# Stepping the start addresses of the activation buffers in a two-layer decoder trunk

## The chip, the cores and the metric

The kernel runs on one NeuronCore of a Trainium2 chip. Its five engines are TensorE (PE in the profile, with its weight loads shown apart as PEld), VectorE (DVE), ScalarE (ACT), GpSimd (POOL) and SyncE (SP). The metric is the device time of one execution in microseconds (us), given as the median over several runs.

## What is computed

The reference is a trunk of two decoder layers over 256 tokens of width 2048. Layer 0 mixes tokens by retention (8 heads), layer 1 by sliding-window attention (32 query heads, 4 key heads). A gated convolutional feed-forward block follows each:

```python
def reference(x, ...):
    h = x
    for i in range(DEPTH):
        hn = rmsnorm(h, norm_mix_g[i])
        h = h + (retention(...) if i % 2 == 0 else sliding_window_attention(...))
        hn = rmsnorm(h, norm_ffn_g[i])
        h = h + conv_ffn(hn, ffn_w_up[i], ffn_conv_w[i], ffn_conv_b[i], ffn_w_down[i])
    return rmsnorm(h, final_norm_g)
```

All of it is float32. Nearly all the arithmetic is in the products of 256 tokens with weight matrices: 2048 x 12288 and 4096 x 2048 for retention, 2048 x 2560 and 2048 x 2048 for attention, and 2048 x 11008 and 5504 x 2048 in each feed-forward block.

## The kernel before

Each float32 operand of a large product is split into a high part and a remainder, so that a product becomes three matmuls in TensorE's fast float32 type: high by high, high by remainder, remainder by high.

**Weights.** A unit of weights is 1 MB (128 partitions x 2048 floats, a few chunks of 128 rows side by side). A DMA from SyncE brings it into one of three `raw` buffers. ScalarE copies it to `hi` (line 156) and VectorE writes the remainder to `lo` (line 157), four buffers of each, in pieces of 1024 columns. `run_main` walks through the units in one fixed order, loads five units ahead and splits about three ahead.

**Activations.** They are held transposed, a chunk of 128 features by 256 tokens at a time, high part and remainder side by side: 512 floats, 2048 bytes in each partition. The norm's chunks are the 16 buffers `xT`, made in `halves` (lines 306 and 310). The gated chunks of the feed-forward blocks are 18 buffers `zT`, made at the end of `ffn_tile` (lines 596 to 600). The mixers' output chunks are `yT`.

**Two forms of the product.** `products` (lines 243 to 245) has the activation as stationary operand: a weight load reads 128 of its columns, 512 bytes of each partition, and the matmul then streams 512 columns of `hi` or `lo`. It serves the down-projections, the output projections and the retention's values and gates. `products_tr` (lines 254 and 256) has it the other way round: 128 columns of `hi` or `lo` are loaded as stationary operand, and the activation streams past. For each chunk of activations this is a block of four matmuls: two of 512 columns (line 254) and two of 256 (line 256). It serves queries, keys and the up-projections. In attention, line 380 loads 64 columns of the values `vs` as stationary operand (`vc` picks them: the first of two heads at a multiple of 512 bytes, the second 256 bytes past one) and streams 256 or 128 columns of `pT`.

**Where buffers lie.** The pools are laid out one above the other in each partition: constants, `acts` (the `xT` buffers), `wp` (`raw`, `hi`, `lo`), `st` (small tiles), and a pool per phase (`zT`, `yT`, `u`, `cv`, the heads' tiles). A tile `free` of 40 floats, which nothing uses, stands at the end of the constants. In the program as built, every buffer of `xT`, `zT`, `yT`, `raw`, `hi` and `lo` starts at a multiple of 512 bytes, and so do the slices that weight loads and matmuls of the two product forms read.

Of the kernel before, what the change touches and what calls it, by code (L numbers as in the profile page):

```python
# [9 lines left out]
F32 = mybir.dt.float32  # L10
F32R = mybir.dt.float32r
# [5 lines left out]
P = 128  # L17
D = 2048
S = 256
NT = S // P  # L20
NC = D // P
# [86 lines left out]
class Kernel:  # L108
# [178 lines left out]
    def squares(self, p):  # L287
# [8 lines left out]
                nc.gpsimd.tensor_tensor(out=self.acc, in0=self.acc, in1=sq[:, i], op=ALU.add)  # L296
        yield 0

    def halves(self, norm, at):

        nc = self.nc
        made = []
        for c, src in at:
            g = self.gT[:, norm * NC + c : norm * NC + c + 1]
            x = self.acts.tile([P, 2, S], F32R, tag="xT", name="xT", bufs=NC)
            nc.scalar.activation(out=x[:, 0], in_=src, func=AF.Copy, scale=g)
            made.append((src, g, x))
            self.xT[c] = x
        for src, g, x in made:
            nc.vector.scalar_tensor_tensor(  # L310
                out=x[:, 1], in0=src, scalar=g, in1=x[:, 0].bitcast(F32),
                op0=ALU.mult, op1=ALU.subtract,
            )
# [261 lines left out]
    def ffn_tile(self, zT, layer, f, u):  # L575
        nc = self.nc
        c = self.ph.tile([P, 2, S], F32, tag="cv", name="cv", bufs=2)
        for half in range(2):
            w = self.cw[:, layer, f + half * NF]
            nc.scalar.activation(  # L580
                out=c[:, half], in_=u[:, half], func=AF.Identity, scale=w[:, 2:3], bias=w[:, 3:4]
            )
        yield 1
        for half in range(2):
            w = self.cw[:, layer, f + half * NF]
            for d in (1, 2):
                nc.vector.scalar_tensor_tensor(  # L587
                    out=c[:, half, d:], in0=u[:, half, : S - d], scalar=w[:, 2 - d : 3 - d],
                    in1=c[:, half, d:], op0=ALU.mult, op1=ALU.add,
                )  # L590
        yield 1
        nc.scalar.activation(out=c[:, 0], in_=c[:, 0], func=AF.Silu)
        yield 1
        s = c[:, 0]
        nc.vector.tensor_tensor(out=s, in0=s, in1=c[:, 1], op=ALU.mult)
        z = self.ph.tile([P, 2, S], F32R, tag="zT", name="zT", bufs=18)
        nc.scalar.copy(out=z[:, 0], in_=s)
        if f + 1 not in F_CUTS:
            yield 1
        nc.vector.tensor_tensor(out=z[:, 1], in0=s, in1=z[:, 0].bitcast(F32), op=ALU.subtract)  # L600
        zT[f] = z
# [190 lines left out]
    def run(self):  # L792
        nc, a, const = self.nc, self.a, self.const
        self.ph_ctx = None
        self.ident = const.tile([P, P], F32, name="ident")
        make_identity(nc, self.ident)
        self.ones = const.tile([P, P], F32, name="ones")
        nc.gpsimd.memset(self.ones, 1.0)
        self.mhalf = const.tile([P, NT], F32, name="mhalf")
        nc.gpsimd.memset(self.mhalf, -0.5)  # L800
        nc.scalar.copy(out=self.mhalf, in_=self.mhalf)
        self.h = const.tile([P, NC, S], F32, name="h")
        self.htok = self.h.rearrange("p c (t d) -> p t c d", t=NT)
        self.gT = const.tile([P, 4 * NC], F32, name="gT")
        nc.sync.dma_start(out=self.gT, in_=a["gT"])
        self.cw = const.tile([P, 2, 2 * NF, 4], F32, name="cw")
        self.bT = const.tile([P, 18], F32, name="bT")
        self.bv = const.tile([P, 256], F32, name="bv")
        self.sinks = const.tile([P, KV * GRP], F32, name="sinks")

        const.tile([P, 40], F32, name="free")

        self.plan_retention()
        self.plan_ffn(0)
        self.plan_attention()
        self.plan_ffn(1)

        self.open_phase("ret")
        self.units[0].groups[0].begin = None
        for c0, c1, n in ((0, 2, 1), (2, 4, 3), (4, 8, 4), (8, 12, 6), (12, 16, 7)):  # L820
            nc.sync.dma_start(out=self.h[:, c0:c1], in_=a["xT"][:, c0:c1])
            self.load_to(n)
        for p, n in ((0, 1), (1, 3), (2, 4), (3, 4)):
            self.norm_halves(0, p)
            self.split_to(n)
        for p, at in enumerate(NORM_AT, 4):
            self.add(self.norm_pair(0, p), at)
        for p in range(NC // 2):
            self.add(self.squares(p), SQUARES[0] + p * SQUARES[1])
        self.add(self.norm_scale(2), SCALE_AT)  # L830
        self.add(self.constants(), 2)
        self.add(self.tokens(), TOKENS_AT)
        self.run_main()
        self.ph_ctx.close()
# [107 lines left out]
```

## Time and profile before

| | |
|---|---|
| median of 3 runs | 2447.19 us (2446.1 to 2448.56) |
| the profiled execution | 2445.04 us, span 2442.9 us |
| granted TensorE clock, mean | 0.998 |
| PE busy | 2425.2 us, 99% of the span |
| DVE, ACT, POOL busy | 64%, 50%, 1% |
| DMA engines busy, by slice of the span | 4 to 7 tenths, 188 GB/s |

The span goes from the first instruction to the last. A matmul's recorded duration is longer than its share of the engine's time, since matmuls overlap; what a matmul costs is read from the distance between the starts of two that follow each other. PEld rows are weight loads, which run beside the matmul before them.

### The profile page before, as it was taken

To read this page: it belongs to the slowest core of one execution; us is meant where nothing else is said; L and a number is where in the kernel's file an instruction comes from. 1 tells how busy PE (TensorE), PEld (TensorE's weight loads), DVE (VectorE), ACT (ScalarE), POOL (GpSimd) and SP (SyncE) were. 2 spreads that over 40 slices of the span, in tenths; PEclk is the share of its full clock that TensorE was granted. 3 is DMA by queue.
4 is the path that set the end of the run, shared out by engine and by line. 5 is a ranking of instruction groups with operands and counts; after the bars stand their busy time and mean duration, and the time that the engine had idled before them with its cause. 6 is when DMAs were issued, how large, how long until landed. Compare 5 with 4: busy or idle time off the path is not lost.

```text
span 2442.9 us, 31366 instructions
## 1 busy us (share of the span) xinstructions
PE 2425.2 (99%) x12676; PEld 2063.1 (84%) x12676; DVE 1554.8 (64%) x2104; ACT 1225.2 (50%) x1782; POOL 28.9 (1%) x37
## 2 busy tenths in 40 slices
PE   8999999999999999999999999999999999999998
PEld 6888888888888888888888888888888888888887
DVE  6555555554556775677577756876777477657774
ACT  5444344344445553555455545765555355535553
POOL 3000000000000000000000000000000000000000
PEclk9999999999999999999999999999999999999999
DMA  7655555555554555555555555445555555554553
GB/s 270 218 185 185 184 189 180 187 187 182 181 194 168 196 183 193 193 191 180 199 191 192 191 184 193 182 155 194 174 190 174 206 190 190 190 206 174 192 199 127
DMA packets 68977, 460.27 MB, mean 188 GB/s; under 512 B 8032, under 2 KB 9184, under 8 KB 16736
## 3 DMA queue, kind: packets, MB, share of 16 engines
q1 hardware_dynamic: 68544, 457.23, 52.6%
q8 instruction: 99, 1.62, 0.3%
q10 hardware_dynamic: 288, 1.05, 0.1%
q14 instruction: 46, 0.38, 0.0%
HBM read 456.15 MB, written 2.10 MB: 188 GB/s over the span
## 4 chain that ended last, share of the span: by engine, by line
PE 97%; DMA 1%; POOL 1%; issue 1%; ACT 0%; DVE 0%; POOLq 0%; SPq 0%; ACTq 0%
PE mm L254 33%; PE mm L256 17%; PE mm L243 15%; PE mm L245 15%; PE mm L244 15%; PE po L380 1%; PE ms L263 1%; DMA raw<-in_ret_in 1%; PE ms L665 1%; POOL acc L296 1%; PE ms L489 0%; DMA h<-in_xT 0%; DVE lo L157 0%; PE ms L354 0%; ACT hi L156 0%
## 5 line engine op out<-in xcount | busy, mean ns | idle before, releaser
L157 DVE TENSOR_TENSOR lo<-raw,hi 128x1024 fp32r<-128x1024 f32 (+1 forms) x849 | 1017.2, 1217 | 601.2 <-ACT hi L156 600.8
L254 PE MATMUL mm<-xT,hi 128*128 128x512 f32 x3552 | 1120.5, 397 | 6.2 <-DVE xT L310 6.2
L156 ACT CAST hi<-raw 128x1024 fp32r<-128x1024 f32 (+1 forms) x849 | 858.0, 1042 | 514.3 <-PE mm L245 290.8
L256 PEld LDWEIGHTS mm<-xT,lo 128*128 128x128 f32 x3552 | 667.7, 188 | 159.5 <-DVE lo L157 2.2
L256 PE MATMUL mm<-xT,lo 128*128 128x256 f32 x3552 | 699.3, 278 | 0.6 <-DVE lo L157 0.6
L254 PEld LDWEIGHTS mm<-xT,hi 128*128 128x128 f32 x3552 | 543.7, 189 | 11.6 <-ACT hi L156 6.2
L243 PE MATMUL mm<-hi,zT 128*128 128x512 f32 x688 | 268.3, 390 | 0.0
L245 PE MATMUL mm<-hi,zT 128*128 128x512 f32 x688 | 267.7, 389 | 0.0
L244 PE MATMUL mm<-lo,zT 128*128 128x512 f32 x688 | 267.7, 389 | 0.0
L243 PE MATMUL mm<-hi,xT 128*128 128x512 f32 (+1 forms) x544 | 212.0, 390 | 2.1 <-DVE q L366 2.1
L245 PE MATMUL mm<-hi,xT 128*128 128x512 f32 (+1 forms) x544 | 209.1, 384 | 0.0
L244 PE MATMUL mm<-lo,xT 128*128 128x512 f32 (+1 forms) x544 | 209.1, 384 | 0.0
L587 DVE SCALAR_TENSOR_TENSOR cv<-u,cw,cv 128x255 f32<-128x255 f32 x344 | 158.3, 481 | 6.1
L243 PE MATMUL mm<-hi,yT 128*128 128x512 f32 x384 | 153.2, 399 | 0.0
L245 PEld LDWEIGHTS mm<-hi,zT 128*128 128x128 f32 x688 | 129.1, 188 | 26.9
L243 PEld LDWEIGHTS mm<-hi,zT 128*128 128x128 f32 x688 | 129.1, 188 | 26.5
L244 PEld LDWEIGHTS mm<-lo,zT 128*128 128x128 f32 x688 | 129.2, 188 | 26.4
L245 PE MATMUL mm<-hi,yT 128*128 128x512 f32 x384 | 149.8, 390 | 0.0
L244 PE MATMUL mm<-lo,yT 128*128 128x512 f32 x384 | 149.7, 390 | 0.0
L365 ACT COPY u<-mm 128x512 f32<-128x512 f32 x86 | 50.4, 586 | 192.9 <-PE mm L256 192.9
L366 DVE TENSOR_TENSOR u<-mm,u 128x512 f32<-128x512 f32 x86 | 59.5, 692 | 101.8 <-ACT u L365 101.8
L243 PEld LDWEIGHTS mm<-hi,xT 128*128 128x128 f32 x544 | 102.7, 189 | 21.9 <-DVE q L366 2.3
(112 smaller groups left out, 1402.5 us busy)
## 6 DMA issues: line engine op xcount, KB each, us to landing
raw<-in_up SPq DMA_DIRECT2D x172, 1024.0 KB, 4.7
raw<-in_ret_in SPq DMA_DIRECT2D x94, 1024.0 KB, 4.7
raw<-in_dn SPq DMA_DIRECT2D x72, 1024.0 KB, 4.8
raw<-in_ret_out SPq DMA_DIRECT2D x32, 1024.0 KB, 4.7
raw<-in_qkv SPq DMA_DIRECT2D x20, 1024.0 KB, 4.7
raw<-in_att_out SPq DMA_DIRECT2D x14, 1024.0 KB, 4.8
raw<-in_dn SPq DMA_DIRECT2D x16, 512.0 KB, 3.3
raw<-in_dn SPq DMA_DIRECT2D x8, 768.0 KB, 4.3
```

The source lines that it names most:

```text
L156: nc.scalar.copy(out=hi, in_=raw)
L157: nc.vector.tensor_tensor(out=lo, in0=raw, in1=hi.bitcast(F32), op=ALU.subtract)
L243: nc.tensor.matmul(out, lhsT=ah, rhs=hi, start=first, stop=False)
L244: nc.tensor.matmul(out, lhsT=ah, rhs=lo, start=False, stop=False)
L245: nc.tensor.matmul(out, lhsT=al, rhs=hi, start=False, stop=last)
L254: nc.tensor.matmul(out, lhsT=hi[:, sl], rhs=both, start=first, stop=False)
L256: nc.tensor.matmul(out[:, :S], lhsT=lo[:, sl], rhs=act[:, 0], start=False, stop=last)
L263: self.nc.tensor.transpose(out=ps[:, j * P : (j + 1) * P], in_=x, identity=self.ident)
L296: nc.gpsimd.tensor_tensor(out=self.acc, in0=self.acc, in1=sq[:, i], op=ALU.add)
L365: nc.scalar.copy(out=x, in_=g.ps[:, :, S:])
L366: nc.vector.tensor_tensor(out=x, in0=g.ps[:, :, :S], in1=x, op=ALU.add)
L587: nc.vector.scalar_tensor_tensor(out=c[:, half, d:], in0=u[:, half, : S - d], scalar=w[:, 2 - d : 3 - d], in1=c[:, half, d:], op0=ALU.mult ...
```

## The change

Each `xT` and each `zT` buffer is made 4 floats (16 bytes) longer than its 512 floats, and the kernel uses the first 512 of them. A tile `gap` of 64 floats (256 bytes) is set ahead of the `xT` buffers. The scratch memory for software-generated DMA descriptors is cut from 16,384 to 1,024 bytes a partition, which frees the room.

```diff
+    def stepped(self, pool, tag, bufs):
+
+        x = pool.tile([P, 2 * S + 4], F32R, tag=tag, name=tag, bufs=bufs)
+        return x[:, : 2 * S].rearrange("p (x s) -> p x s", x=2)
...
-            x = self.acts.tile([P, 2, S], F32R, tag="xT", name="xT", bufs=NC)
+            x = self.stepped(self.acts, "xT", NC)
...
-        z = self.ph.tile([P, 2, S], F32R, tag="zT", name="zT", bufs=18)
+        z = self.stepped(self.ph, "zT", 18)
...
         const.tile([P, 40], F32, name="free")
+        self.acts.tile([P, 64], F32, name="gap")
...
-    nc = bacc.Bacc("TRN2", target_bir_lowering=False, num_devices=1)
+    nc = bacc.Bacc(
+        "TRN2", target_bir_lowering=False, num_devices=1, dynamic_dma_scratch_size=1024
+    )
```

The instructions of every engine, their order and their waits are the same in both programs. Only addresses differ. In the program as built the pool rounds each buffer up to a multiple of 32 bytes, so that the 2064 bytes take 2080, and neighbours are 32 bytes further past a multiple of 512, not 16. Addresses below are bytes within a partition; the residue is what is left over a multiple of 512:

```
buffers        first address, residue, pitch before    first address, residue, pitch after
xT (16)            41472      0       2048                 26368     256       2080
raw (3)            74240      0       8192                 59648     256       8192
hi (4)             98816      0       8192                 84224     256       8192
lo (4)            131584      0       8192                116992     256       8192
zT (18)           178688      0       2048                164096     256       2080
yT, attention     204288      0       2048                189696     256       2048
```

After the change, then, all buffers of weights start 256 bytes past a multiple of 512, and the k-th `xT` or `zT` buffer starts 32k bytes further round than they do: the first at the same residue as the weights, the next 32 bytes on, and so on round the circle of 512 once in 16 buffers. `yT` keeps the residue of the weights.

## Rows read from the trace of the kernel before

**Rows 1.** The page, part 1: busy time, share and instructions.
```profile
PE 2425.2 (99%) x12676; PEld 2063.1 (84%) x12676; DVE 1554.8 (64%) x2104; ACT 1225.2 (50%) x1782; POOL 28.9 (1%) x37
```

**Rows 2.** The page, part 4: chain that ended last, by engine.
```profile
PE 97%; DMA 1%; POOL 1%; issue 1%; ACT 0%; DVE 0%; POOLq 0%; SPq 0%; ACTq 0%
```

**Rows 3.** The waits of PE: total us, times, longest us.
```profile
PE mm L254 <- DVE xT L310: 6.2, 1, 6.2
PE mm L243 <- DVE q L366: 2.1, 1, 2.1
PE mm L256 <- DVE lo L157: 0.6, 2, 0.4
```

**Rows 4.** The page, part 5, groups: busy us, mean ns, idle us before, releaser.
```profile
L157 DVE TENSOR_TENSOR lo<-raw,hi 128x1024 fp32r<-128x1024 f32 (+1 forms) x849 | 1017.2, 1217 | 601.2 <-ACT hi L156 600.8
L254 PE MATMUL mm<-xT,hi 128*128 128x512 f32 x3552 | 1120.5, 397 | 6.2 <-DVE xT L310 6.2
L256 PE MATMUL mm<-xT,lo 128*128 128x256 f32 x3552 | 699.3, 278 | 0.6 <-DVE lo L157 0.6
...
L243 PE MATMUL mm<-hi,zT 128*128 128x512 f32 x688 | 268.3, 390 | 0.0
...
L243 PE MATMUL mm<-hi,xT 128*128 128x512 f32 (+1 forms) x544 | 212.0, 390 | 2.1 <-DVE q L366 2.1
...
L243 PE MATMUL mm<-hi,yT 128*128 128x512 f32 x384 | 153.2, 399 | 0.0
```

**Rows 5.** Windows: us; PE busy (instructions); granted clock; DMA share; GB/s.
```profile
1000.00:1050.00 50.00, 50.00 (x289) 1.00 0.49 170
1160.00:1190.00 30.00, 30.00 (x134) 1.00 0.54 207
```

**Rows 6.** Timeline of PE in an up-projection: start us, recorded us, instructions.
```profile
1000.35 0.63 PE L254 MATMUL mm<-xT,hi 128*128 128x512 f32 x2
1000.82 0.39 PE L256 MATMUL mm<-xT,lo 128*128 128x256 f32 x2
1001.04 0.63 PE L254 MATMUL mm<-xT,hi 128*128 128x512 f32 x2
1001.51 0.40 PE L256 MATMUL mm<-xT,lo 128*128 128x256 f32 x2
1001.74 0.63 PE L254 MATMUL mm<-xT,hi 128*128 128x512 f32 x2
```

**Rows 7.** Timeline of PE in a down-projection.
```profile
1164.93 0.39 PE L243 MATMUL mm<-hi,zT 128*128 128x512 f32 x1
1165.16 0.39 PE L244 MATMUL mm<-lo,zT 128*128 128x512 f32 x1
...
1167.65 0.39 PE L243 MATMUL mm<-hi,zT 128*128 128x512 f32 x1
```

**Rows 8.** Timeline of PE, one pair of attention heads, whole.
```profile
1545.50 1.21 PE L380 MATMUL po<-pT,vs 128*64 128x256 f32 x12
1546.55 0.44 PE L254 MATMUL mm<-xT,hi 128*128 128x512 f32 x1
```

**Rows 9.** The same, from where the second head of the pair starts.
```profile
1546.02 0.69 PE L380 MATMUL po<-pT,vs 128*64 128x256 f32 x6
```

**Rows 10.** Groups of weight loads (128 and 64 columns): busy us, mean ns.
```profile
L245 PEld LDWEIGHTS mm<-hi,zT 128*128 128x128 f32 x688 | 129.1, 188 | 26.9
L380 PEld LDWEIGHTS po<-pT,vs 128*64 128x64 f32 x192 | 19.0, 134 | 1.2
```

**Rows 11.** Window in attention: PE, PEld, DVE, ACT, POOL busy; clock; DMA.
```profile
1550.00:1600.00 50.00, 50.00 (x315) 41.33 (x315) 43.93 (x125) 36.22 (x102) 0.00 (x0) 1.00 0.44 158
```

**Rows 12.** The page, part 3: the DMA queues.
```profile
q1 hardware_dynamic: 68544, 457.23, 52.6%
q8 instruction: 99, 1.62, 0.3%
q10 hardware_dynamic: 288, 1.05, 0.1%
q14 instruction: 46, 0.38, 0.0%
```

**Rows 13.** The chain in order of time: start us, us, longest DMA pieces.
```profile
6.89 5.13 DMA raw<-in_ret_in
...
17.10 10.13 DMA raw<-in_ret_in
```

## The prediction, blind

> **What bounds the kernel now.** I read the busy times first. TensorE is busy 99% of the span, the next engine 64% [rows 1]. The chain that ended last says the same in another way: 97% of it is PE, and every other engine and the DMA have 1% or less each [rows 2]. PE's list of waits shows how little there is to gain from what feeds it: its longest wait in all is one of 6.2 us, the next 2.1 us [rows 3]. So the time is the number of matmuls times the distance between their starts, and a change of addresses counts only if it changes that distance (or makes some feeder so slow that PE waits).
>
> The distance is read from two places. In a down-projection, line 243 starts at 1164.93 and again, twelve matmuls later, at 1167.65 [rows 7]: 2.72 us / 12 = 0.2267 us for each matmul of 512 columns. In an up-projection two blocks of four take from 1000.35 to 1001.74 [rows 6]: 0.695 us for a block of 512 + 512 + 256 + 256 = 1536 columns. In both stretches the clock is granted in full, 1.00, the level of 2.4 GHz [rows 5]. Columns alone, at one per cycle, would be 512 / 2.4 = 213.3 ns and 1536 / 2.4 = 640 ns. What goes beyond them is 13.3 ns for a matmul of the first form and 55 / 4 = 13.8 ns for one of the second, whether it streams 512 columns or 256.
>
> The attention rows tell what this excess goes with. Twelve matmuls there, six of 256 and six of 128 columns, take from 1545.50 to 1546.55 [rows 8]: 1.05 us against 2304 / 2.4 = 960 ns, an excess of 7.5 ns each. Their stationary operand has 64 columns, not 128. Half the weight columns, about half the excess: it looks as if the load of the next weights, which runs beside the matmul, holds the stream up a little. That makes addresses worth asking about, since both reads come from the same memory, and in the kernel before both start at a multiple of 512 bytes in all the large products.
>
> **How much is at stake.** There are 3 x (688 + 544 + 384) = 4848 matmuls of the first form (the counts are those of line 243 [rows 4], and lines 244 and 245 run as often), of which 3 x 384 = 1152 read `yT`, which keeps its place relative to the weights. That leaves 3696. Of the second form there are 3552 / 2 = 1776 blocks [rows 4]. The excess within reach is 3696 x 13.3 ns = 49 us and 1776 x 55 ns = 98 us, together 147 us of 2445.
>
> **The change part by part.**
>
> *The stepped buffers and the gap.* No instruction is added, removed or moved. The pool rounds 2064 bytes up to 2080, so the step is 32 bytes, and the weights move to residue 256. Between a weight slice and the activation buffer it meets, the residue now differs by 32k bytes, with k from 0 to 15, where it was zero. What does that cost or give? The trace of before has no stretch with such a difference at 128 weight columns; the nearest is attention, where the second head's weights lie 256 bytes further round than what they meet, the first head's do not. The second head's six matmuls take from 1546.02 [rows 9] to 1546.55 [rows 8], 0.53 us. The first head's take from 1545.50 to 1546.02, 0.52 us. The two agree within the rows' rounding, and 0.01 us in six, 1.7 ns a matmul, is the most that the difference could be read as.
>
> There is also a reason to expect nothing. A weight load of 128 columns is recorded with 188 ns, one of 64 with 134 [rows 10]: 54 ns for 64 columns, 0.84 ns a column, while the stream takes 0.42 ns. So beside the load of 512 bytes the stream passes through about 1024. The two reads do not run in step: whatever residue they start from, one passes over the other's residues in turn. A different starting point would shift the moment at which they meet, not how often. I take zero, by the row of the two heads, and as bounds: a gain of 147 x 15/16 = 138 us (one buffer in sixteen still stands at the weights' residue), and a loss of 1.7 ns on 15/16 of the 10,800 matmuls concerned, 17 us.
>
> The row's excess stands against a rule. The Trainium skill, in "TensorE: Matmul & The Clock Gate", section "Step-by-step: what each phase is for", says that the weight load and the streamed operand have independent read ports and that loading the next weights takes no read bandwidth from the running matmul. By that, no address could matter and the sum is zero here too; the rows above agree with zero for an offset of 256 bytes, but the excess that falls with the weight columns speaks against the rule as it stands.
>
> *All other engines.* `raw`, `hi` and `lo` now start at residue 256, and ScalarE and VectorE write the stepped buffers. Their instructions could become longer. VectorE's splits have 601.2 us of idle time ahead of them [rows 4], and in the fullest attention window VectorE is busy 43.93 of 50 us and ScalarE 36.22 [rows 11]. Even 10% more on every VectorE instruction there gives 48.3 of 50: covered. Were it more, PE would wait for `lo` in that stretch first.
>
> *The DMA.* The loads land at residue 256. At the start PE does wait for them: pieces of 5.13 and 10.13 us on the chain [rows 13]. If every load took 10% longer, that would be about 1.5 us, under what can be told. In the steady stretches the DMA engines are busy about half the time [rows 5], with loads issued five units ahead, so it is covered.
>
> *The scratch.* It serves DMAs whose descriptors software makes. The queues are four, two of them hardware_dynamic and two for instructions [rows 12]; none would use it. Zero.
>
> **The sum.** 2445.04 us for the profiled execution, plus zero. The median of the runs shown lies 2.15 us above that execution, so the forecast for a median is 2447.2 us.
>
> **The rivals.**
>
> *The reads stop colliding: faster.* For it: the excess goes with the weight columns, and before, both reads begin at the same residue everywhere. Against it: the second head shows no gain at 256 bytes, and the two reads run at different paces. It comes in two sizes. A small one is that only the pacing inside a block improves. Its two matmuls of 512 columns take 1000.35 to 1000.82, 0.47 us [rows 6], against 2 x 0.2267 = 0.453 us in the other form [rows 7]; the same work differs by 17 ns with the company that it is in. Getting that back gives 1776 x 17 ns = 30 us, 2417 us. The large one is the bound above: 138 us less, 2309 us, in which matmuls pace at their columns alone. Between them anything is possible.
>
> The Trainium skill's "TensorE: Matmul & The Clock Gate", section "Back-to-back issue gap", gives for a matmul alone a distance of columns / 2.4 plus 2.5 ns, 216 ns for 512. Estimated with that figure, the concerned matmuls would save 11 ns each, some 119 us, and the time would be 2328 us. No row here shows such a distance in a product.
>
> *Slices across a boundary: slower.* Before, each weight slice of 512 bytes fills exactly one stretch between multiples of 512. After, every slice of `hi`, `lo`, `zT` and `xT` that isn't at residue 0 lies across a multiple. If a read that crosses costs something, or if the residues that differ meet more often than equal ones, PE slows on nearly every matmul. At the 1.7 ns that the two heads leave room for, that is 10,125 x 1.7 ns = 17 us: 2464 us. For it: the second head is, if anything, the slower. Against it: the difference is at the limit of the rows. It decides from 4.9 / 10,125 us, half a nanosecond a matmul.
>
> *The change doesn't do what it says.* It does not, in a sense: the step is 32 bytes and the weights are displaced as well. If only which 16 bytes are read together matters, 32 and 256 change nothing, and the time is that of the forecast; I count this with it.
>
> **How the numbers follow.** About 0.2%, 4.9 us, is what a measurement of this kernel can tell from no change. Since the distance of 10,800 matmuls hangs on addresses, an effect of half a nanosecond each would already leave that band, so the two sides keep much of the chance. Forecast, no dependence on these residues: 0.45. Faster: 0.31, of which 0.19 around the small size and 0.12 for more. Slower: 0.24. The range has the forecast, the small gain with some room (down to 2412) and the loss of 17 us with some room (up to 2470); it leaves out the large gain and a loss beyond the two heads' bound, together about 0.19. The forecast's own range would be 2442 to 2452.
>
> **What would show it right or wrong.** Right: in the profile after, twelve matmuls of a down-projection still take 2.72 us, and two blocks of an up-projection 1.39 us, in every buffer alike, and PE's waits stay under 10 us in sum. The faster rival shows as distances below 0.2267 and 0.695 us in the products that read `xT` and `zT`, while those that read `yT` keep theirs. The slower rival shows as longer distances, in `yT` too if crossing is the cause, and not in `yT` if the differing residues are. Distances that go up and down with the buffer's number would say that the residue matters, whatever the sum. The prediction is wrong if PE's distances change by half a nanosecond or more on average, or if a wait for `hi`, `lo` or a load appears on PE that the list of before doesn't have.

## The result and the profile after

The changed kernel takes 2468.23 us (2467.84 to 2468.5, 4 runs) against 2446.64 us of the kernel before (4 runs): a ratio of 1.0088, 95% interval 1.0076 to 1.0101. It is slower by 21.6 us. The time lies in the stated range; the forecast of no change was not the case that came, the slower rival (2464 us) was.

TensorE is as busy in share as before [rows 1], and longer in time. The page of the kernel after, part 1 and the chain by engine:

```profile
PE 2446.0 (99%) x12676; PEld 2071.3 (84%) x12676; DVE 1555.8 (63%) x2104; ACT 1225.2 (50%) x1782; POOL 28.6 (1%) x37
...
PE 97%; DMA 1%; POOL 1%; issue 0%; ACT 0%; DVE 0%; SPq 0%; POOLq 0%; DVEq 0%; ACTq 0%
```

PE is busy 20.8 us longer with the same 12,676 matmuls; VectorE and ScalarE take what they took. The list of PE's waits after (total us, times, longest us) has grown by some 2 us in sum against [rows 3], and its longest is 6.3 us where it was 6.2:

```profile
PE mm L254 <- DVE xT L315: 6.3, 1, 6.3
PE mm L243 <- DVE q L371: 2.2, 1, 2.2
PE mm L256 <- DVE lo L157: 1.6, 3, 0.5
PE ms L344 <- POOL acc L296: 1.1, 1, 1.1
```

So the matmuls themselves stand further apart. The page of the kernel after, part 5, groups that answer to [rows 4] (busy us, mean ns, idle us before):

```profile
L157 DVE TENSOR_TENSOR lo<-raw,hi 128x1024 fp32r<-128x1024 f32 (+1 forms) x849 | 1017.9, 1218 | 620.5 <-ACT hi L156 619.9
...
L254 PE MATMUL mm<-xT,hi 128*128 128x512 f32 x3552 | 1111.2, 394 | 6.4 <-DVE xT L315 6.3
...
L256 PE MATMUL mm<-xT,lo 128*128 128x256 f32 x3552 | 709.3, 281 | 1.6 <-DVE lo L157 1.6
L243 PE MATMUL mm<-hi,zT 128*128 128x512 f32 x688 | 272.0, 395 | 0.0
...
L243 PE MATMUL mm<-hi,xT 128*128 128x512 f32 (+1 forms) x544 | 214.4, 394 | 2.2 <-DVE q L371 2.2
...
L243 PE MATMUL mm<-hi,yT 128*128 128x512 f32 x384 | 153.2, 399 | 0.0
```

The reader should compare the recorded means. A matmul on `zT` has gone from 390 to 395 ns, one on `xT` from 390 to 394. One on `yT`, which was displaced with the weights and keeps its place relative to them, has 399 before and 399 after. In the second form, the busy time of line 254 falls by 9.3 us and that of line 256 rises by 10.0: the two nearly cancel. VectorE's splits are as long as before.

The timeline of PE in a down-projection after, to be read against [rows 7]:

```profile
1169.99 0.39 PE L243 MATMUL mm<-hi,zT 128*128 128x512 f32 x1
...
1172.78 0.40 PE L243 MATMUL mm<-hi,zT 128*128 128x512 f32 x1
```

Twelve matmuls take 2.79 us, 232.5 ns each, where they took 2.72 us, 226.7 ns.

**Where the 22.8 us between the two spans went.** The starts of all matmuls in the two traces give the mean distances, breaks over 330 ns left out. The first form on `zT`: 232.69 ns against 227.06, 2064 x 5.63 ns = 11.6 us. On `xT`, those of 512 columns: 233.16 against 227.63, 1536 x 5.53 ns = 8.5 us. The second form: line 254's distances are 2.72 ns shorter and line 256's 2.87 ns longer, 3552 x 0.15 ns = 0.5 us. PE's waits: some 2 us. Together 22.6 us.

Set beside the addresses of the built program, the same distances show a pattern. Means over the changed kernel, breaks left out, by the residue of the activation buffer relative to the weights; a block is the four matmuls of the second form:

```
residue (bytes)   block, ns (before: 696.9)   first form on zT, ns (before: 226.8)
      0                 696.2                       229.3
     32                 692.7                       232.8
     64                 688.5                       233.7
     96                 705.9                       232.9
    128                 700.0                       231.9
    160                 702.9                       234.7
    192                 691.1                       231.7
    224                 698.3                       233.3
    256                 697.3                       230.2
    288                 692.9                       232.6
    320                 690.0                       233.0
    352                 705.7                       233.1
    384                 700.4                       232.7
    416                 701.8                       234.8
    448                 692.0                       232.3
    480                 698.9                       233.5
```

A block costs between 688 and 706 ns. The second half of the column repeats the first, so the residue counts, and the mean is near the value before. In the first form, every residue is worse than 226.8 ns, 0 and 256 too, although these two cost nothing where all buffers share them (below): what stands around a buffer counts as well.

### The profile page after: what moved, and what is told of

It reads as the page before. It is cut to its first block, busy times and chain, and to the rows that moved or that the text cites. A ratio compares the mean times of both kernels' runs of the same rounds, so it can differ in the third digit from the quotient of the medians.

```text
span 2465.7 us, 31366 instructions
## 1 busy us (share of the span) xinstructions
PE 2446.0 (99%) x12676; PEld 2071.3 (84%) x12676; DVE 1555.8 (63%) x2104; ACT 1225.2 (50%) x1782; POOL 28.6 (1%) x37
## 4 chain that ended last, share of the span: by engine, by line
PE 97%; DMA 1%; POOL 1%; issue 0%; ACT 0%; DVE 0%; SPq 0%; POOLq 0%; DVEq 0%; ACTq 0%
PE mm L254 33%; PE mm L256 17%; PE mm L243 15%; PE mm L245 15%; PE mm L244 15%; PE po L385 1%; PE ms L263 1%; DMA raw<-in_ret_in 1%; PE ms L670 1%; POOL acc L296 1%; PE ms L494 0%; DMA h<-in_xT 0%; DVE lo L157 0%; PE ms L359 0%; ACT hi L156 0%
## 5 line engine op out<-in xcount | busy, mean ns | idle before, releaser
L256 PE MATMUL mm<-xT,lo 128*128 128x256 f32 x3552 | 709.3, 281 | 1.6 <-DVE lo L157 1.6
L243 PE MATMUL mm<-hi,zT 128*128 128x512 f32 x688 | 272.0, 395 | 0.0
L245 PE MATMUL mm<-hi,zT 128*128 128x512 f32 x688 | 271.7, 395 | 0.0
L243 PE MATMUL mm<-hi,xT 128*128 128x512 f32 (+1 forms) x544 | 214.4, 394 | 2.2 <-DVE q L371 2.2
L245 PE MATMUL mm<-hi,xT 128*128 128x512 f32 (+1 forms) x544 | 211.8, 389 | 0.0
```

Source lines behind the costliest of these rows:

```text
L243: nc.tensor.matmul(out, lhsT=ah, rhs=hi, start=first, stop=False)
L245: nc.tensor.matmul(out, lhsT=al, rhs=hi, start=False, stop=last)
L256: nc.tensor.matmul(out[:, :S], lhsT=lo[:, sl], rhs=act[:, 0], start=False, stop=last)
```

## The experiments

Theory, formed from the profile after: the distance between matmuls depends on the residue of the weight slice relative to the streamed operand. Rival: what costs is that slices cross a multiple of 512. Further rivals: that neighbouring buffers differ at all, or that the smaller scratch or the displacement of everything else does it.

### The displacement without the step

```diff
-        x = pool.tile([P, 2 * S + 4], F32R, tag=tag, name=tag, bufs=bufs)
+        x = pool.tile([P, 2 * S], F32R, tag=tag, name=tag, bufs=bufs)
```

> Only the step is taken out: the gap and the small scratch stay, xT and zT are 2048 bytes apart again, so all buffers lie 256 bytes past a multiple of 512 and every weight slice still crosses a multiple, but each at the same residue as what it meets. Theory (the residue of the weight slice relative to the streamed operand sets the distance): as before, 2446.6 us within 3 us, 226.8 ns a matmul of 512 columns on zT. Rival (slices across a multiple of 512 cost): as the change, 2463 to 2470 us, with zT and yT products alike at 231 to 233 ns. If the scratch or the shift of everything else is behind the loss, 2468 us too.

Measured: 2446.5 us, ratio 1.0003 (0.9994 to 1.0012). Distances: 226.79 ns on `zT`, 696.8 ns a block. Crossing a multiple of 512, the gap and the scratch are out: all slices cross here, and nothing is lost.

### The step on one kind of buffer alone

```diff
-            x = self.stepped(self.acts, "xT", NC)
+            x = self.acts.tile([P, 2, S], F32R, tag="xT", name="xT", bufs=NC)
```

> Only zT is stepped by 32 bytes, xT is flat at the residue of the weights. Theory: 2064 matmuls on zT cost 5.9 ns more each, 12 us: 2459 us (2456 to 2461), blocks of the up-projection at 697 ns on average and xT products at 227 ns as before. Rival (slices across a multiple): 2468 us.

```diff
-        z = self.stepped(self.ph, "zT", 18)
+        z = self.ph.tile([P, 2, S], F32R, tag="zT", name="zT", bufs=18)
```

> Only xT is stepped. Theory: 1536 matmuls of 512 columns on xT in the first form cost 5.7 ns more each, 9 us, and the blocks of the second form come out nearly even over the sixteen residues, 1 ns each, 2 us: 2457 to 2458 us (2455 to 2460), zT products at 226.8 ns. Rival (slices across a multiple): 2468 us; rival (the second form carries the loss): over 2462 us.

Measured: 2458.95 us with `zT` stepped, ratio 1.0050 (1.0038 to 1.0063), and 2456.05 us with `xT` stepped, ratio 1.0038 (1.0026 to 1.0051). The losses of 12.6 and 9.7 us add up to some 22 us, that of the whole change being 21.6. The page of the run with `zT` alone stepped, part 5, shows the cost only where the step is:

```profile
L243 PE MATMUL mm<-hi,zT 128*128 128x512 f32 x688 | 272.1, 395 | 0.0
...
L243 PE MATMUL mm<-hi,xT 128*128 128x512 f32 (+1 forms) x544 | 212.0, 390 | 2.4 <-DVE q L371 2.4
```

and that of the run with `xT` alone stepped shows the reverse:

```profile
L243 PE MATMUL mm<-hi,zT 128*128 128x512 f32 x688 | 268.2, 390 | 0.0
...
L243 PE MATMUL mm<-hi,xT 128*128 128x512 f32 (+1 forms) x544 | 214.7, 395 | 1.6 <-DVE q L371 1.6
```

The means of 395 and 390 ns change places; the two costs are separate and simply add.

### The step, 16 bytes on

```diff
-        x = pool.tile([P, 2 * S + 4], F32R, tag=tag, name=tag, bufs=bufs)
-        return x[:, : 2 * S].rearrange("p (x s) -> p x s", x=2)
+        x = pool.tile([P, 2 * S + 8], F32R, tag=tag, name=tag, bufs=bufs)
+        return x[:, 4 : 2 * S + 4].rearrange("p (x s) -> p x s", x=2)
```

> As the change, with the xT and zT operands 16 bytes further in their buffers, so that the residues relative to the weights are 16, 48, 80 and so on, and never 0. A map of the residues between those of the change. Theory: zT products between 230 and 236 ns at every residue, the loss of the change without its one good buffer in sixteen: 2466 to 2476 us. If only equal 16-byte lines matter and nothing finer, the values lie between those of the neighbours of the change; if residues that are odd multiples of 16 are free of the loss, 2447 us.

Measured: 2469.87 us, ratio 1.0094 (1.0080 to 1.0108). The blocks at odd multiples of 16 bytes run from 686.2 ns (residue 112) to 710.8 ns (208), and again the same 256 bytes further: 686.5 at 368, 709.2 at 464. They do not lie between their neighbours of the first map (705.9 and 700.0 stand around 686.2), so 32 bytes are too coarse to read the pattern. The `zT` products lie between 227.3 (residue 496) and 233.3 ns, where the forecast had all of them at 230 or more.

### One residue for all buffers

Is it the residue, or that neighbours differ? In these kernels no buffer is stepped: buffers are 2560 bytes apart and the operand starts `o` floats into its buffer, the weights at a multiple of 512. The small scratch of the change stays in all of them (not shown in the cuts); the first experiment had shown it to cost nothing. For `zT` by 32 bytes:

```diff
-        z = self.ph.tile([P, 2, S], F32R, tag="zT", name="zT", bufs=18)
+        z = self.ph.tile([P, 2 * S + 128], F32R, tag="zT", name="zT", bufs=18)
+        z = z[:, 8 : 8 + 2 * S].rearrange("p (x s) -> p x s", x=2)
```

> zT alone is displaced, every buffer by the same 32 bytes, so that neighbours do not differ among each other and only the relation to the weights is broken. Theory: 2064 matmuls at about 232.7 ns instead of 226.8, 12 us more: 2458 us (2455 to 2462). Rival (what costs is that neighbouring buffers differ): 2446 us.

Measured: 2462.63 us, ratio 1.0058 (1.0045 to 1.0070), just above the forecast's 2455 to 2462. A timeline of PE in a down-projection of this run:

```profile
1164.65 0.40 PE L245 MATMUL mm<-hi,zT 128*128 128x512 f32 x1
...
1167.45 0.40 PE L245 MATMUL mm<-hi,zT 128*128 128x512 f32 x1
```

Twelve in 2.80 us, 233.3 ns each: the loss needs no differing neighbours, only the wrong relation to the weights. The stationary operand's address alone was moved here. Nor does the operand run into another engine's accesses: by the starts in this trace, the mean is 233.3 ns on the 517 matmuls beside which VectorE and ScalarE are idle, on the 1335 beside which one of them is busy throughout (233.35), and on the 676 during which no DMA packet is in flight.

For `xT`, the buffers of the first norm stay at the residue of the weights (they are stationary operands in retention), those of the three others move (shown for 112 bytes; 64 and 208 have 16 and 52 in place of 28):

```diff
-            x = self.acts.tile([P, 2, S], F32R, tag="xT", name="xT", bufs=NC)
+            x = self.acts.tile([P, 2 * S + 128], F32R, tag="xT", name="xT", bufs=NC)
+            o = 0 if norm == 0 else 28
+            x = x[:, o : o + 2 * S].rearrange("p (x s) -> p x s", x=2)
```

> No step: all xT buffers of the second, third and fourth norm stand at one residue, 112 bytes past that of the weights; those of the first norm (retention, which uses xT as stationary operand), zT and yT stand at the residue of the weights. Theory (the residue alone sets the distance): the blocks of the second form, 1520 of 1776, take the 686 ns that the run with 16 more bytes showed at residue 112 instead of 697, 16 us less: 2430 us (2427 to 2434). Rival (a distance belongs to a pattern of stepped neighbours, and a constant offset brings nothing): 2446 us.

> As the run at 112, with residue 64, where the change itself showed 688.5 ns a block: 1520 blocks x 8.4 ns = 13 us less, 2434 us (2430 to 2437). Rival (pattern of neighbours): 2446 us.

> As the run at 112, with residue 208, the dearest of the map for the second form (710.8 ns a block): 1520 x 14 ns = 21 us more, 2468 us (2463 to 2471). Rival (pattern of neighbours): 2446 us.

Measured: at 112 bytes 2448.02 us, ratio 1.0003 (0.9994 to 1.0012), a miss; at 64 bytes 2438.47 us, ratio 0.9961 (0.9949 to 0.9974), faster than both kernels, though 1.5 us outside the 2430 to 2437 forecast; at 208 bytes 2466.33 us, ratio 1.0077 (1.0061 to 1.0092), as forecast. The timeline of PE in an up-projection at 64 bytes:

```profile
1000.29 0.62 PE L254 MATMUL mm<-xT,hi 128*128 128x512 f32 x2
...
1001.67 0.62 PE L254 MATMUL mm<-xT,hi 128*128 128x512 f32 x2
```

and at 208 bytes:

```profile
1000.00 0.63 PE L254 MATMUL mm<-xT,hi 128*128 128x512 f32 x2
...
1001.42 0.63 PE L254 MATMUL mm<-xT,hi 128*128 128x512 f32 x2
```

Two blocks take 1.38 and 1.42 us, against 1.39 before [rows 6]. Over the whole trace a block costs 690.6 ns at 64, 710.1 at 208 and 697.9 at 112. The first two agree with the maps (688.5, 710.8), the third does not (686.2). In the stepped kernel a chunk's neighbours stood 32 bytes to either side. The relation of the two operands alone does not fix a block's pace: in the trace at 112 bytes, blocks with the same relation take 690, 696 and 707 to 708 ns in turn, over and over; at 64 bytes 687 or 688 and 692 or 693 alternate, at 208 bytes 706 or 707 and 713 or 714. So a block's pace also hangs on the one ahead of it. How, is not settled.

### More residues

```diff
-            o = 0 if norm == 0 else 28
+            o = (0, 48, 8, 14)[norm]
```

> A map of constant residues, one per norm, zT and yT at the weights' residue: xT of the first feed-forward block at 192, of attention at 32, of the second feed-forward block at 56 bytes (the one value here that is no multiple of 16). If a constant residue paces as the stepped map says: 691 ns a block at 192, 693 at 32, and some 2440 us. If what the neighbouring chunk's residue was counts as well, as the run at 112 suggests (698 ns instead of 686), single values may lie up to 12 ns off, either way: 2430 to 2452 us.

Measured, in one run: 2446.2 us beside 2445.63 of the kernel before, so not the 2440 that the stepped map gave. A block costs 693.4 ns at 192 bytes and 702.1 at 56. The attention blocks at 32 (701.2) are few and often interrupted.

```diff
+        self.wp.tile([P, 16], F32, tag="gap", name="gap", bufs=1)
...
-        z = self.ph.tile([P, 2, S], F32R, tag="zT", name="zT", bufs=18)
+        z = self.ph.tile([P, 2 * S + 128], F32R, tag="zT", name="zT", bufs=18)
+        o = (64, 124)[layer]
+        z = z[:, o : o + 2 * S].rearrange("p (x s) -> p x s", x=2)
```

> A second map: the weights and everything above them 64 bytes further up, so that all xT buffers stand at 448 relative to them; zT at 256 in the first layer and at 496 in the second. If the stepped map holds: 692 ns a block, 230 to 232 ns a matmul on xT in the first form, 230 on zT in layer 0 and 227.3 in layer 1, the sum 2446 to 2452 us. If one of these beats 226.8 ns, equal residues are not the best for the first form.

Measured, in one run: 2445.7 us beside 2445.63. A block at 448 bytes costs 693.9 ns, as at 192, which is 256 less. The first form takes 226.82 ns on `zT` at 256 bytes, 226.69 at 496, and 229.0 on `xT` at 448, each less than the stepped maps had (230.2, 227.3 and 232.3). Equal residues, those 256 bytes apart and 496 are alike; none clearly beats equal ones.

```diff
-            o = (0, 48, 8, 14)[norm]
+            o = (0, 36, 12, 32)[norm]
```

> Three more constant residues of xT, one per norm: 144 bytes in the first feed-forward block, 48 in attention, 128 in the second. By the stepped map 694, 700 and 700 ns a block, but the constant residues have differed from it by up to 12 ns. A value under 690.6 ns would beat the 64 bytes of the faster version; I expect none: 2444 to 2452 us.

Measured, in one run: 2447.7 us beside 2446.18; 698.0 ns a block at 144, 696.7 at 128, and 700 at 48 in the few unbroken blocks of attention. The 64 bytes stay the best constant tried.

Two of these means hide two paces. At 144 bytes, the up-projection's blocks ahead of the first down-projection take 693.6 ns and the 464 after it 700.0, with the same residue and the same instructions. At 56 bytes the two are 706.5 and 700.0. The timeline of PE at 144 bytes, in a stretch ahead and one after, both at a granted clock of 1.00:

```profile
890.17 0.61 PE L254 MATMUL mm<-xT,hi 128*128 128x512 f32 x2
...
897.10 0.61 PE L254 MATMUL mm<-xT,hi 128*128 128x512 f32 x2
...
1000.44 0.63 PE L254 MATMUL mm<-xT,hi 128*128 128x512 f32 x2
...
1007.44 0.63 PE L254 MATMUL mm<-xT,hi 128*128 128x512 f32 x2
```

Ten blocks take 6.93 us in the first and 7.00 us in the second. One offset can thus settle at either of two paces; what decides between them is not shown.

### The step, 256 bytes

```diff
-        x = pool.tile([P, 2 * S + 4], F32R, tag=tag, name=tag, bufs=bufs)
+        x = pool.tile([P, 2 * S + 64], F32R, tag=tag, name=tag, bufs=bufs)
```

> The change with a step of 256 bytes in place of 32: every buffer differs from its neighbour, every other one stands 256 bytes away from the weights' residue. Theory (the pattern repeats every 256 bytes): 2446.5 us, 227 ns a matmul, 697 ns a block. Rival (any step costs, or the pattern repeats at 512): 2452 us or more, with every other chunk slower.

Measured: 2447.36 us, ratio 1.0003 (0.9994 to 1.0012). The distances are 226.81 and 226.76 ns on `zT` at residues 0 and 256, and 696.2 and 697.5 ns a block. A step of 256 bytes costs nothing.

## Why the forecast was wrong and the range right

**What bounds the kernel: right.** The time moved with the distance between matmuls and with little else: VectorE and ScalarE are busy as long as before within 1 us, and PE's waits grew by some 2 us, to 11.2 (the prediction's sign was under 10). Steps costed at nothing (the other engines, the DMA, the scratch) were nothing: the kernel with the displacement and the small scratch but without the step is level with the one before.

**The excess goes with the weight load: not shown.** The prediction read from attention that about half the excess goes with half the weight columns. But attention's matmuls also stream fewer columns. By the starts in the trace of before, matmuls of 256 columns stand 115 to 116 ns apart with 64 weight columns (line 380) and with 128 (line 256; two of them take 0.22 to 0.23 us in [rows 6]), where their columns alone would take 106.7: half the weight columns, the same excess. The 13.8 ns "whether it streams 512 columns or 256" are a mean of some 20 and 9. So it was in part luck that this lead pointed at addresses. What the runs do bear out is that the relation between the two operands of a matmul counts: moving only the stationary operand (`zT` by 32 bytes) or only the streamed one in the second form (`xT` by 64 or 208) changes the pace, and moving both together by 256 does not.

**The step that failed** is the argument for zero: "A different starting point would shift the moment at which they meet, not how often." It was backed by the row of the two attention heads, which differ by 256 bytes and pace alike [rows 8, 9]. The step of 256 bytes shows why that row could say nothing: at 256 bytes the pattern of the large products has come round to its start. In the first form it is the one offset, of those the change makes, that costs as little as zero (230.2 and 229.3 ns). The recorded paces of load and stream do differ [rows 10], yet the effect does not average out: a matmul of the first form costs 226.8 ns at equal residues and 233.3 at 32 bytes, on average over every buffer alike. With it came the sign of being wrong that the prediction had named, a change of half a nanosecond a matmul: 20.6 us over its 10,800 matmuls are 1.9 ns.

**The rule on the weight load.** The Trainium skill's "TensorE: Matmul & The Clock Gate", section "Step-by-step: what each phase is for", has the next weights' load take no read bandwidth from the running matmul. The runs do not fit it: at a granted clock of 1.00, the pace of the matmuls hangs on where one of the operands lies relative to the other, by up to 20 ns a block of four, and here the measurement decides. Whether it is the load's reading that holds the stream up was not measured by itself.

**The slower rival** came, in one of its two forms and with another sum. "If a read that crosses costs something" is refuted by the displacement without the step. "If the residues that differ meet more often than equal ones" holds for the first form: 3600 matmuls at 5.5 to 5.6 ns, 20 us, where the rival had 10,125 at 1.7 ns, 17 us. That the two sums are near each other is chance: the loss is three times as large on a third of the matmuls, while the second form, the larger part of the work, came out even. The sign that was named for this form, longer distances on `zT` and `xT` and none on `yT`, is what the profile shows, and the distances go up and down with the buffer's number, as they would where the residue matters.

**The faster rivals.** A gain was there for the second form, 6 ns a block at 64 bytes, but not by stepping, which visits good and bad residues alike. The small price in the prediction, 17 ns a block and 30 us, was too high: the kernel with one good residue for three of the four norms gains 1520 x 6.2 ns = 9.4 us by its block means, and 8.2 us by the medians. The large gain, matmuls at their columns alone, appeared at no residue tried.

**Not doing what it says.** The 32 bytes in place of 16 do not decide: residues at odd multiples of 16 have good and bad values too (686.2 to 710.8 ns a block).

## What to carry to other kernels

Where a kernel is bound by back-to-back matmuls, the addresses of the two operands relative to each other are a parameter, worth here a gain of 0.4% or a loss of 0.9%. Try one constant offset at a time, separately for each form of product, and read the distance between starts rather than the total, in more than one stretch, since the pace at one offset can differ between them. Stepping buffers through many offsets mixes good with bad, and it loses outright where the offset that all buffers had was the best one. A reading that tests an address effect at a single offset can sit on the period of the pattern, as the 256 bytes did here.

## What the runs showed of the hardware that was not expected

- The distance between matmuls of this float32 type, at a granted clock of 1.00 (2.4 GHz), depends on the operands' relative addresses within a partition: 226.8 ns (equal, or 256 bytes apart) to 233.3 ns (32 bytes apart) for a constant residue in the first form, 690.6 to 710.1 ns for a block of the second.
- The pattern repeats every 256 bytes, in both forms: 693.4 and 693.9 ns at 192 and 448, 226.8 ns at 0 and 256. The absolute address made no difference: all operands moved together by 256 bytes pace as before, and so does `yT` in the run at 448, where it and its weights were moved together by 64 bytes (227.7 ns in both kernels).
- It has structure below 32 bytes: as constants, 56 and 64 bytes cost 702.1 and 690.6 ns a block.
- The relation does not fix the pace alone: at 112 bytes blocks of 690, 696 and 708 ns take turns, and at 144 bytes one stretch runs at 693.6 ns a block and another at 700.0.
- The best relation differs with the form: of those tried, equal residues (and 256 and 496 bytes, which are alike) when the activation is stationary, 64 bytes when the weights are.
- What in the memory or the engine makes the pattern is not shown. That the weight load and the stream collide fits the rows, but no run measured the two apart. VectorE, ScalarE and the DMA are not what it hangs on (233.3 ns with and without them, first form at 32 bytes). Nor is it known how a block's pace hangs on the one before, which would be needed to say why 112 bytes are good in the step and not as a constant.
